# Moving the place at which split weights begin inside their tiles

## The chip, the cores and the metric

The kernel runs on one core of one Trainium2 chip. The number that counts is the device time of one execution in microseconds; three runs of the kernel before gave 1131.67, 1130.79 and 1130.77 us, so the median is 1130.79 us. A separate execution was profiled; everything that is said of single instructions comes from it. Its own time was 1131.15 us, of which 1129.4 us lie between the first and the last instruction.

## The reference

A decoder trunk of two layers on 512 tokens with 1024 features. Layer 0 mixes with a gated delta rule (six heads, chunks, short convolutions), layer 1 with sliding-window attention (twelve heads, sinks); both layers also attend to 256 memory tokens. After each mixer comes an output projection and a gated feed-forward part. Cut to what this case touches:

```python
def swiglu(h, w_gate_up, w_down):
    gu = h @ w_gate_up
    return (jax.nn.silu(gu[..., :D_FF]) * gu[..., D_FF:]) @ w_down

for layer in range(DEPTH):
    h = rms_norm(x, ln_mix[layer])
    ...                                   # mixer: projections of h, recurrence or attention
    x = x + jnp.concatenate([mix_out, mem_o], axis=-1) @ w_out[layer]
    x = x + swiglu(rms_norm(x, ln_ffn[layer]), w_gate_up[layer], w_down[layer])
    if layer == N_A_LAYERS - 1:
        kv = rms_norm(x, ln_kv) @ w_kv    # keys and values that layer 1 reads
return rms_norm(x, ln_final)
```

Here `D_MODEL` is 1024, `D_FF` is 2816, and all arrays are 32-bit floats. Nearly all arithmetic is in products of the activations with weight matrices.

## The kernel before

Activations are kept transposed: features on the 128 partitions, the 512 tokens along the free dimension. Every float32 operand of a large product is split into two parts, `h` (rounded to the type float32r, written by ScalarE at line 140) and `l` (the rest, written by VectorE at line 153), and one product becomes three matrix instructions, `whi` by `h`, `whi` by `l` and `wlo` by `h` (`mm3`, line 198). In each of them a 128 by 128 block of weights is loaded into TensorE and the activation streams past it.

There are two kinds of weights.

Whole projection tiles. `weight` (line 182) loads 128 output columns of a matrix, 1024 rows deep, as a tile of 128 by 1024 (two tiles of 768 and 640 in the down projection), splits it into a pair of tiles tagged `whi` and `wlo`, and `mm3` uses 512 bytes of a partition, 128 numbers, at a time. The activations that stream past are 512 tokens wide. 2478 matrix instructions of the program are of this kind. The tiles rotate over three buffers, so the next pair is split while the last one is used. The pair of tiles is 1152 numbers wide (`part`, line 195: `D + P`), 128 more than a weight needs, and a projection's weights begin at the first number.

Quarter weights. In the feed-forward part, the gate and up projections of two column tiles are computed together by a scheme with seven products for eight (`quarters`, line 1275): weights and activations are cut into halves, sums of the halves are formed by DMAs with addition, VectorE and ScalarE, and seven products of a 128 by 512 block of weights with 256 tokens follow, each of twelve matrix instructions. Nineteen such groups a layer, 38 in all, make 38 x 7 x 12 = 3192 matrix instructions. Their split weights go to a ring of six places (`ring`, line 1131): three pairs of tiles, two places in each, 512 numbers apart. Each place is a view of 512 numbers within the tile that begins `shift[0]` numbers after the place's start; `begin` sets `shift[0]` to `P - 8`, that is 120 numbers or 480 bytes, before its first product. Two places share one tile, so a place that is written with another shift can overlap its neighbour.

Tiles of 128 by 512 and 128 by 1024 are multiples of 512 bytes a partition, so in the built program the projections' weights and the activations they meet begin at the same position within a block of 512 bytes, and the quarter weights begin 480 bytes further on. In this document that difference, the weights' start less the activation's start within 512 bytes, is called the lag: 0 for the projections and 480 for the quarters. In the first 32 us, memory keys and values are made from other tiles and with lags of 128 and 384. At the end of layer 1 (from 1103.66 us) the last output tiles are made in pieces of 256 tokens with a lag of 0.

A scheduler orders each engine's instructions from the program's order and its dependences. Two views of one tile depend on each other when their bytes overlap. Each engine runs its own list in order.

Of the kernel before, what the change touches and what calls it, by code (L numbers as in the profile page):

```python
# [18 lines left out]
P = 128  # L19
# [8 lines left out]
FT = DFF // P  # L28
# [58 lines left out]
class Builder:  # L87
    def __init__(self, tc, a):
        self.tc, self.nc, self.a = tc, tc.nc, a
        self.n = 0  # L90
        self.valued, self.turned, self.scaled, self.behind = None, [], None, None
        self.scalings = []
        self.table, self.table_ins, self.table_users = None, None, []


# [86 lines left out]
    def weight(self, src, eng=None, raw=None, parts=1, pool=None, tags=("whi", "wlo"), bufs=3, after=None):  # L182

        raw = self.load(src) if raw is None else raw
        n = raw.shape[1]
        hi, lo = (self.part(tag, bufs, pool)[:, :n] for tag in tags)
        for i in range(parts):
            s = slice(i * n // parts, (i + 1) * n // parts)
            self.split(raw[:, s], hi[:, s], lo[:, s], eng or self.weng)
            if after is not None:  # L190
                for ins, other in zip((self.copied, self.low), after):
                    self.nosync(ins, other)
        return hi, lo
# [905 lines left out]
    def ffn(self, fp, xp, layer, h, apool, rope=False):  # L1099
# [4 lines left out]
        acts, sums, open_pairs, places, waiting, shift, sized = [], [], [], [], [], [0], []  # L1104
# [34 lines left out]
        def begin(f, up, by, tag, bufs, then):  # L1139

            o = [self.t(fp, [P, T], F32, tag, bufs) for _ in range(2)]
            steps = self.quarters(fp, [col(f + i, up) for i in range(2)], sums, by, o, ring)
            shift[0] = P - 8
            next(steps)
            while waiting:
                x = waiting.pop()
                self.nosync(self.fn(x, x, AF.Silu), self.held)
            end()
            next(steps)
            open_pairs.append((steps, then, o))  # L1150
            return o

        def end():
            if open_pairs:
                steps, then, o = open_pairs.pop()
                next(steps, None)
                for x in o:
                    then(x)
# [8 lines left out]
        for f0 in (0, half):  # L1167
# [7 lines left out]
            for f in range(f0 + 1, f0 + half, 2):  # L1175
                if f == 1:
                    g = []
                    for i in range(2):
                        for _ in range(2 - i):
                            sums.append(self.token_sums(fp, layer, len(sums), h))  # L1180
                        g.append(gate(f + i))
                    sums.append(self.token_sums(fp, layer, len(sums), h))
                else:
                    g = begin(f, 0, (self.rstd, self.rstd), "fg", 4, lambda x: self.fn(x, x, AF.Silu))
                begin(f, 1, g, "fu", 3, put)
# [432 lines left out]
```

## Time and profile before

| | |
|---|---|
| median of three runs | 1130.79 us |
| profiled execution | 1131.15 us, span 1129.4 us |
| TensorE (PE) busy | 1119.9 us, 99% of the span, 7339 instructions |
| weight loads (PEld) busy | 986.1 us, 87% |
| VectorE (DVE) busy | 827.6 us, 73% |
| ScalarE (ACT) busy | 634.4 us, 56% |
| granted TensorE clock | 0.998 |

An instruction of TensorE shows as two records, a weight load on the row PEld and a product on the row PE. Products are pipelined: the record of a 512-wide one lasts about 0.39 us, though the next starts some 0.23 us after it. So the duration in a row is no cost; what a matrix instruction costs is the distance from its start to the next start, and this document reads pace from start times. In the view by stretches, "x" counts the instructions that touch a stretch.

### The profile page before, as it was taken

What the parts mean: (1) busy time and instruction counts of PE and PEld (TensorE: products, weight loads), DVE (VectorE), ACT (ScalarE), POOL (GpSimd) and SP (SyncE); (2) the same over time, 40 slices, a digit from 0 to 9 for tenths busy, and PEclk for the clock granted to TensorE, in tenths of its full rate; (3) what the DMA queues carried; (4) which work ended last, traced back from release to release, by engine and by line L of the source; (5) the groups of instructions that cost most, each with busy time, mean ns of one, the idle gap of its engine ahead of it and who ended that gap; (6) DMA issues with size and microseconds to landing.
All of it is one profiled execution on the core that took longest, in us unless ns stands there. A gap on an engine that the chain in (4) does not pass through costs nothing.

```text
span 1129.4 us, 19330 instructions
## 1 busy us (share of the span) xinstructions
PE 1119.9 (99%) x7339; PEld 986.1 (87%) x7339; DVE 827.6 (73%) x1553; ACT 634.4 (56%) x1285; POOL 73.2 (6%) x91
## 2 busy tenths in 40 slices
PE   9999999999999999999999999999999999999997
PEld 8888778887899988899988887788999988999986
DVE  7676976577888975588955877839999634889643
ACT  8588664456566632366643555856666422666434
POOL 0000000000021001011000000000111000111001
PEclk9999999999999999999999999999999999999999
DMA  8344252234567536377533321116687533776232
GB/s 314 109 153 149 95 131 86 85 113 145 174 167 195 143 111 169 102 191 195 134 89 102 132 75 38 53 43 180 158 201 185 144 103 105 173 190 156 77 103 87
DMA packets 72401, 151.15 MB, mean 134 GB/s; under 512 B 16956, under 2 KB 18516, under 8 KB 72308
## 3 DMA queue, kind: packets, MB, share of 16 engines
q1 hardware_dynamic: 60884, 129.21, 36.3%
q0 software_dynamic: 11136, 20.45, 11.2%
q8 instruction: 57, 0.93, 0.3%
q14 instruction: 36, 0.29, 0.1%
q10 hardware_dynamic: 288, 0.26, 0.1%
HBM read 142.94 MB, written 6.96 MB: 133 GB/s over the span
## 4 chain that ended last, share of the span: by engine, by line
PE 96%; DVE 2%; ACT 1%; DMA 0%; issue 0%; DVEq 0%; SPq 0%; ACTq 0%
PE pj L146 46%; PE g L146 38%; PE sc L146 6%; PE qk L146 3%; PE pt L146 2%; PE pt L150 1%; PE g L150 1%; DVE big L153 1%; DVE qv L156 0%; DVE btmp L153 0%; DMA early<-in_early 0%; DVE wlo L153 0%; ACT sm L134 0%; DVE T L153 0%; DVE gcr L153 0%
## 5 line engine op out<-in xcount | busy, mean ns | idle before, releaser
L140 ACT ACTIVATE whi<-wraw 128x512 fp32r<-128x512 f32 (+3 forms) x318 | 235.3, 748 | 240.6 <-PE pj L146 164.0
L153 DVE TENSOR_TENSOR wlo<-wraw,whi 128x512 fp32r<-128x512 f32 (+3 forms) x318 | 262.8, 837 | 92.7 <-ACT whi L140 85.2
L146 PE MATMUL pj<-h,whi 128*128 128x512 f32 (+1 forms) x652 | 256.4, 395 | 0.0
L146 PE MATMUL pj<-l,whi 128*128 128x512 f32 (+1 forms) x652 | 254.4, 390 | 0.0
L146 PE MATMUL pj<-h,wlo 128*128 128x512 f32 (+1 forms) x652 | 254.0, 390 | 0.0
L146 PE MATMUL g<-T,whi 128*128 128x256 f32 x1216 | 216.8, 279 | 0.0
L146 PEld LDWEIGHTS g<-T,whi 128*128 128x128 f32 x1216 | 185.1, 188 | 1.3 <-DVE fu L156 1.3
L146 PE MATMUL g<-T,wlo 128*128 128x256 f32 x608 | 169.7, 279 | 0.0
L146 PEld LDWEIGHTS pj<-h,whi 128*128 128x128 f32 x652 | 122.4, 188 | 28.0 <-issue 4.1
L146 PEld LDWEIGHTS pj<-h,wlo 128*128 128x128 f32 x652 | 122.5, 188 | 25.4 <-issue 0.9
L146 PE MATMUL g<-l,whi 128*128 128x256 f32 (+1 forms) x500 | 144.5, 289 | 0.0
L146 PE MATMUL g<-h,whi 128*128 128x256 f32 (+1 forms) x500 | 144.4, 289 | 0.0
L146 PE MATMUL g<-h,wlo 128*128 128x256 f32 (+1 forms) x500 | 144.4, 289 | 0.0
L146 PEld LDWEIGHTS pj<-l,whi 128*128 128x128 f32 x652 | 122.6, 188 | 23.6 <-DVE l L1468 0.3
L146 PEld LDWEIGHTS g<-T,wlo 128*128 128x128 f32 x608 | 114.3, 188 | 0.0
L146 PEld LDWEIGHTS g<-h,whi 128*128 128x128 f32 x500 | 94.0, 188 | 1.9
L146 PEld LDWEIGHTS g<-l,whi 128*128 128x128 f32 x500 | 93.9, 188 | 1.9
L146 PEld LDWEIGHTS g<-h,wlo 128*128 128x128 f32 x500 | 93.9, 188 | 1.8
L1286 POOL DMA_DIRECT2D ws<-in_wgu x38 | 33.5, 881 | 733.0 <-DMA ws<-in_wgu 399.1
L140 ACT ACTIVATE whi<-ws 128x512 fp32r<-128x512 f32 x76 | 48.0, 631 | 42.0 <-PE g L146 35.6
L153 DVE TENSOR_TENSOR wlo<-ws,whi 128x512 fp32r<-128x512 f32 x76 | 52.0, 684 | 5.9 <-ACT whi L140 5.9
L1287 POOL DMA_DIRECT2D ws<-in_wgu x38 | 34.2, 900 | 196.4 <-DVE wlo L153 71.4
(421 smaller groups left out, 1683.2 us busy)
## 6 DMA issues: line engine op xcount, KB each, us to landing
wraw<-in_wgu SPq DMA_DIRECT2D x50, 512.0 KB, 4.4
ws<-in_wgu SPq DMA_DIRECT2D x76, 256.0 KB, 3.4
ws<-in_wgu POOLq DMA_DIRECT2D x76, 256.0 KB, 4.5
wraw<-in_win SPq DMA_DIRECT2D x26, 512.0 KB, 3.6
wraw<-in_wdn SPq DMA_DIRECT2D x32, 384.0 KB, 3.1
wraw<-in_wdn SPq DMA_DIRECT2D x32, 320.0 KB, 2.9
wraw<-in_wgu SPq DMA_DIRECT2D x38, 256.0 KB, 4.0
wraw<-in_wout SPq DMA_DIRECT2D x16, 512.0 KB, 3.6
```

The costliest lines, as they stand in the source:

```text
L140: self.copied = self.nc.scalar.activation(out, in_, AF.Copy, **kw).ins
L146: return self.nc.tensor.matmul(out, lhsT, rhs, start=start, stop=stop, skip_group_check=more).ins
L150: return self.nc.tensor.transpose(out, in_, self.ident[:k, :k]).ins
L153: return eng.tensor_tensor(out=out, in0=a, in1=b, op=op).ins
L1286: nc.gpsimd.dma_start(s1, a22, accum_op=ALU.add)
L1287: nc.gpsimd.dma_start(s3, a21, accum_op=ALU.add)
```

## The change

Two things move, and nothing else is edited. In `weight`, a projection's split weights now begin `at` numbers into their tiles; `at` is 0 for the first four tiles that are made, 8 for the next four, and so on up to 120, and then 0 again: 32 bytes more each four tiles. Tiles of a pool of their own keep their start. In `begin`, the shift of the quarter weights is 80 numbers (320 bytes) for all 19 groups of layer 0, and in layer 1 16, 24, 84, 76, 112 and 48 numbers for three groups each and 48 for the last.

In terms of the lag: of the 2478 matrix instructions of whole projections, 2412 get a lag other than 0, in steps of 32 bytes from 32 to 480. The 1596 quarter instructions of layer 0 go from 480 to 320. Those of layer 1 go to 64 (240 instructions), 96 (252), 336 (264), 304 (240), 448 (252) and 192 (348).

```diff
-        self.scalings = []
+        self.scalings, self.cuts, self.pairs = [], 0, 0
...
         raw = self.load(src) if raw is None else raw
         n = raw.shape[1]
-        hi, lo = (self.part(tag, bufs, pool)[:, :n] for tag in tags)
+        at = 0
+        if pool is None:
+            at = self.cuts // 4 * 8 % P
+            self.cuts += 1
+        hi, lo = (self.part(tag, bufs, pool)[:, at:at + n] for tag in tags)
...
             steps = self.quarters(fp, [col(f + i, up) for i in range(2)], sums, by, o, ring)
-            shift[0] = P - 8
+            shift[0] = 80 if self.pairs < FT - 3 else (16, 24, 84, 76, 112, 48, 48)[(self.pairs - FT + 3) // 3]
+            self.pairs += 1
             next(steps)
```

The engines' lists are the same before and after, but for a few swaps of neighbours in layer 1. The largest stands in the second half of layer 1, where the shift falls from 112 to 48 between the two places of one tile, `whi_10071`. The names are: `g` the accumulators, `T` and `h` halves of activations and their sums, `whi` and `wlo` the ring's tiles. On TensorE the piece of the difference reads:

```order
 L146 MATMUL g_10710<-T_8392,wlo_10072 128x256
+L146 MATMUL g_10710<-T_8283,whi_10067 128x256
+L146 MATMUL g_10710<-T_8284,whi_10067 128x256
 L146 MATMUL g_10839<-h_8032,whi_10071 128x256
 L146 MATMUL g_10839<-l_8033,whi_10071 128x256
+L146 MATMUL g_10841<-T_8283,whi_10067 128x256
+L146 MATMUL g_10841<-T_8284,whi_10067 128x256
+L146 MATMUL g_10841<-T_8283,wlo_10068 128x256
```

The product into `g_10839` was the next one after that of `g_10710`; now two instructions of another product stand between them, and nine more (the first three are shown) stand after its first two. On ScalarE, at the same place:

```order
 L140 ACTIVATE fs_10777<-g_10710 128x256
-L140 ACTIVATE whi_10069<-wraw_10829 128x512 x2
+L140 ACTIVATE whi_10069<-wraw_10829 128x512
 L140 ACTIVATE h_10889<-fu_10698 128x512
+L140 ACTIVATE whi_10071<-wraw_10829 128x512
+L140 ACTIVATE whi_10069<-wraw_10829 128x512
```

The copy that fills the second place of `whi_10071` stood seven rows earlier and now comes after the product that reads the first place, with which it shares 64 columns.

## Prediction

> **What bounds the kernel now.** I read the page from the top: busy shares, the slices with the granted clock, the chain that ended last.
>
> ```profile
> PE 1119.9 (99%) x7339; PEld 986.1 (87%) x7339; DVE 827.6 (73%) x1553; ACT 634.4 (56%) x1285; POOL 73.2 (6%) x91
> PEclk9999999999999999999999999999999999999999
> PE 96%; DVE 2%; ACT 1%; DMA 0%; issue 0%; DVEq 0%; SPq 0%; ACTq 0%
> PE pj L146 46%; PE g L146 38%; PE sc L146 6%; PE qk L146 3%; PE pt L146 2%; PE pt L150 1%; PE g L150 1%; DVE big L153 1%; DVE qv L156 0%; DVE btmp L153 0%; DMA early<-in_early 0%; DVE wlo L153 0%; ACT sm L134 0%; DVE T L153 0%; DVE gcr L153 0%
> ```
>
> TensorE holds 96% of the chain, 46% with projections (`pj`) and 38% with quarters and a few others (`g`), at a full clock. So a nanosecond more or less per matrix instruction goes almost whole into the time. Next, the pace, from stretches that hold one kind of instruction (the columns are time, then busy time and count of PE, PEld, DVE, ACT, POOL, then clock and DMA):
>
> ```profile
> 320.00:400.00 80.00, 80.00 (x688) 80.00 (x687) 72.86 (x132) 51.24 (x99) 12.22 (x14) 1.00 0.69 170
> 475.00:570.00 95.00, 95.00 (x806) 94.56 (x805) 82.70 (x148) 59.52 (x115) 13.10 (x15) 1.00 0.64 159
> 414.50:466.00 51.50, 51.50 (x229) 42.65 (x228) 31.84 (x48) 12.42 (x16) 3.68 (x4) 1.00 0.52 144
> 33.00:47.00 14.00, 14.00 (x62) 11.40 (x61) 9.19 (x15) 4.14 (x7) 2.39 (x4) 1.00 0.38 132
> ```
>
> The first two are quarter products: about 686 starts in 80 us (688 less those that only reach in), 116.7 ns each, and the same in 95 us. The third is a down projection, 512 tokens wide: 226.7 ns. VectorE, ScalarE and the DMAs are busy in all of them, and the pace doesn't waver, so it isn't set by them. The fourth is also 512 wide, but groups with lags 0 and 288 alternate: 14.39 us over 62 is 232 ns. It is the only long stretch that shows 512-wide products with another lag.
>
> How many instructions there are follows from groups by form:
>
> ```profile
> L146 PE MATMUL g<-T,whi 128*128 128x256 f32 x1216 | 216.8, 279 | 0.0
> L146 PE MATMUL g<-T,wlo 128*128 128x256 f32 x608 | 169.7, 279 | 0.0
> L146 PE MATMUL g<-l,whi 128*128 128x256 f32 x456 | 127.3, 279 | 0.0
> L146 PE MATMUL g<-h,whi 128*128 128x256 f32 x456 | 127.3, 279 | 0.0
> L146 PE MATMUL g<-h,wlo 128*128 128x256 f32 x456 | 127.3, 279 | 0.0
> ```
>
> That is 3192 quarter instructions, as the code has it. Now the pace by lag; each pair of rows is the first and last start of an unbroken run.
>
> ```profile
> 330.97 0.40 PE L146 MATMUL g<-T,whi 128*128 128x256 f32 x2
> 332.37 0.28 PE L146 MATMUL g<-h,whi 128*128 128x256 f32 x1
> ...
> 1104.02 0.28 PE L146 MATMUL pj<-h,whi 128*128 128x256 f32 x1
> 1107.50 0.28 PE L146 MATMUL pj<-ac10h,wlo 128*128 128x256 f32 x1
> ...
> 18.08 0.28 PE L146 MATMUL sc<-mh,wlo 128*128 128x256 f32 x1
> 20.60 0.28 PE L146 MATMUL sc<-mh,wlo 128*128 128x256 f32 x1
> ...
> 29.92 0.28 PE L146 MATMUL pj<-whi,ml 128*128 128x256 f32 x1
> 32.17 0.28 PE L146 MATMUL pj<-wlo,mh 128*128 128x256 f32 x1
> ```
>
> 256 wide: lag 480, 12 steps in 1.40 us, 116.7 ns. Lag 0 (the pieces at the end), 29 steps in 3.48 us, 120.0 ns. Lag 128, 21 steps in 2.52 us, 120.0 ns. Lag 384, 19 steps in 2.25 us, 118.4 ns. So the place seems to matter, by up to 3.3 ns, and the quarters now stand at the best of the four lags that the trace shows.
>
> 512 wide there is a second thing to see, at lag 0:
>
> ```profile
> 649.42 0.40 PE L146 MATMUL pj<-l,whi 128*128 128x512 f32 x1
> 651.74 0.39 PE L146 MATMUL pj<-h,wlo 128*128 128x512 f32 x1
> 654.69 0.39 PE L146 MATMUL pj<-h,whi 128*128 128x512 f32 x1
> ...
> 421.68 0.39 PE L146 MATMUL pj<-h,whi 128*128 128x512 f32 x1
> 429.16 0.39 PE L146 MATMUL pj<-h,whi 128*128 128x512 f32 x1
> ```
>
> After a break the first ten steps take 2.32 us, 232 ns each; the next thirteen 2.95 us, 226.9; and in the down projection 33 steps take 7.48 us, 226.7. The stream of products is restless first and then settles, and a restless product costs 5.3 ns more. Ten of them cost 0.05 us.
>
> **The change, part by part.** It removes and adds no instruction; it moves addresses. What could cost is the copy and subtraction that write the weights, the pace of TensorE, and waits.
>
> Writing at another place I cost at nothing. The quarter weights, written 480 bytes into the block, take as long as activations written at its start:
>
> ```profile
> L153 DVE TENSOR_TENSOR wlo<-wraw,whi 128x512 fp32r<-128x512 f32 x190 | 127.6, 688 | 16.9 <-ACT whi L140 12.1
> L153 DVE TENSOR_TENSOR l<-fu,h 128x512 fp32r<-128x512 f32 x32 | 21.9, 686 | 2.1 <-ACT h L140 1.0
> L140 ACT ACTIVATE whi<-wraw 128x512 fp32r<-128x512 f32 x190 | 116.8, 627 | 63.1 <-PE g L146 41.7 <-PE pj L146 14.3 <-DVE wraw L153 3.2
> L140 ACT ACTIVATE h<-fu 128x512 fp32r<-128x512 f32 x32 | 20.3, 633 | 19.9 <-DVE fu L153 11.8 <-DVE fu L156 8.1
> ```
>
> 688 against 686 ns, and 627 against 633. Both engines wait for TensorE in these stages, so 10 ns more would be covered; were that cover gone, 190 copies would cost 2 us.
>
> Quarters of layer 0, lag 320, 1596 instructions: no row has this lag. The nearest is 384, 118.4 ns; I take 1.8 ns more than now, 2.9 us. The ends are 120.0 ns (5.3 us more) and, since nothing shows that 480 is the best of all lags, as much the other way (5.3 us less).
>
> Quarters of layer 1: lags 64 and 192 (588 instructions) lie next to 0 and 128, both 120.0 ns: 3.3 ns more, 1.9 us. Lags 96, 336 and 304 (756) I give the 1.8 ns of lag 384: 1.4 us. Lag 448 (252) lies between 384 and 480: 0.9 ns, 0.2 us. Together 3.5 us; ends 5.3 us more and 5.3 us less.
>
> Projections, 2412 instructions at a lag other than 0. If a stream at any lag settles as at lag 0, they cost nothing. If at other lags it doesn't, each costs 5.3 ns, 12.8 us, which is what the stretch at 33 us looks like. That stretch changes lag every few instructions, whereas a place now holds for four tiles, some 100 instructions, ten times what settling took. I take a third of them as restless: 4.3 us. At each of 31 changes of place the stream may be restless for ten products, 0.05 us: 1.6 us, of which a third is already in; 1.1 us. Sum 5.4 us. The lower end is a gain: lag 0 is the dearest lag 256 wide; were it so 512 wide, other lags would save up to 3.3 ns, 8.0 us.
>
> One wait is added in layer 1, where the shift falls from 112 to 48 within `whi_10071` (the order above). ScalarE's copy must now wait for the last product with `whi` of the neighbour place. TensorE then has one instruction of that product and two of the next, 0.35 us, before it needs the copy, which takes 0.63 us and a handover: about 0.4 us of stop. Behind the copy on ScalarE stand two more copies for products that come over 1 us later, so nothing else is late; VectorE's subtraction, 0.69 us, ends beside the nine instructions that were moved ahead. Bounds 0.2 and 1.0 us. Where the shift rises, a place overlaps one that was used five products earlier, 7 us: free.
>
> Sum: 2.9 + 3.5 + 5.4 + 0.4 = 12.2 us. On the profiled execution's 1131.15 us that is 1143.35; the median of the runs is 0.36 us less, so I predict 1143.0 us.
>
> **The rivals.** Places don't matter. The four lags come from different parts of the program, with other tiles and other neighbours; the spread of 3.3 ns could belong to these. Then only the 0.4 us of the wait are left: 1131.2 us. Against it speaks that lag 480 gives 116.7 ns with every kind of half (`T`, `h`, `l`) and in stretches 150 us apart, so neighbours hardly matter there. The Trainium skill, in "TensorE: Matmul & The Clock Gate" (Step-by-step: what each phase is for), says that TensorE has two independent read ports and that loading the next weights takes no bandwidth from the running product; by that rule the place could not matter and this rival would be right, with the same 1131.2 us. The trace speaks against it as far as 116.7 and 120.0 ns for one shape do.
>
> Other lags are better for the projections. The mechanism: 256 wide, lag 0 costs 3.3 ns more than 480; the 512-wide products run beside the same weight loads, so lag 0 may cost them the same. With the full 3.3 ns on all moved projections (8.0 us less), half the loss on the quarters (3.2 us) and the wait, 1131.15 - 8.0 + 3.2 + 0.4 - 0.36 gives 1126.4 us. It decides if the moved projections run below 226.7 ns by more than the quarters lose: 6.8 us over 2412 is 2.8 ns, or 1.5 ns if the quarters lose half. For it: lag 0 is the worst seen 256 wide. Against it: the only 512-wide stretch with another lag is the slowest.
>
> Nothing settles. Projections at 232 ns throughout and quarters at 120.0: 12.8 + 10.6 + 0.4 on 1130.79 gives 1154.6 us. For it: the stretch at 33 us and two of four lags. Against it: that stretch mixes lags.
>
> **How the numbers follow.** Forecast, both kinds somewhat slower, 1136 to 1150 us: 0.55. Nothing settles: 0.17. Places don't matter: 0.09. Other lags better: 0.19, of which 0.02 ends within 0.2% of the time before. A difference of 0.2%, 2.3 us, is about what a measurement of this kernel can tell from no change. So faster 0.17, same 0.11, slower 0.72. The range goes from 1127 to 1156 us: it takes in the slow case and all but the far part of the fast one, leaving out about a tenth on each side. The likeliest case alone has 1136 (quarters at half their term, projections with only the 31 changes of place) to 1150 (quarters at 120.0 ns, projections two thirds restless).
>
> **What would show it.** Right: quarter runs of twelve in layer 0 that take more than the 1.40 us of now, near 1.42; another length in layer 1 for each place; down projections in which some tiles keep 7.48 us for 33 instructions and others take up to 7.66; near 1018 us a stop of TensorE of some 0.4 us that ScalarE's copy ends. Durations of copies and subtractions would stay within 10 ns. Wrong: quarters at 1.40 us in layer 0, or below; down projections below 7.48 us; or a stop of more than 1 us at places where the shift rises. What would make the forecast fail is that lags 320 and those between 32 and 480 are simply not like the ones I could see.

## The result and the profile after

The changed kernel takes 1142.07 us in the median of three runs (1141.65 to 1143.23), against 1130.79 us before: 1.0099 times as long, with a 95% interval of 1.0076 to 1.0122. The profiled execution has a span of 1140.3 us, 10.9 us more than the 1129.4 us of before. My 1143.0 us is 0.9 us off, and the sum was right. Its terms were not: two errors, each over 5 us, cancelled.

The page of the changed kernel, first busy time, then the chain that ended last:

```profile
PE 1130.1 (99%) x7339; PEld 986.9 (87%) x7339; DVE 828.1 (73%) x1553; ACT 634.8 (56%) x1285; POOL 73.2 (6%) x91
...
PE 96%; DVE 2%; ACT 1%; issue 0%; DMA 0%; DVEq 0%; ACTq 0%
```

TensorE has the same 7339 instructions and is busy 10.2 us longer; VectorE and ScalarE differ by half a microsecond. So the loss lies in the distance between products, as foreseen. The groups of copies and subtractions that write the weights:

```profile
L153 DVE TENSOR_TENSOR wlo<-wraw,whi 128x512 fp32r<-128x512 f32 x190 | 127.9, 688 | 17.0 <-ACT whi L140 12.3
L140 ACT ACTIVATE whi<-wraw 128x512 fp32r<-128x512 f32 x190 | 116.8, 628 | 69.4 <-PE g L146 42.4 <-PE pj L146 17.3 <-DVE wraw L153 3.2
L153 DVE TENSOR_TENSOR wlo<-wraw,whi 128x1024 fp32r<-128x1024 f32 x66 | 80.2, 1219 | 26.6 <-ACT whi L140 26.3
L140 ACT ACTIVATE whi<-wraw 128x1024 fp32r<-128x1024 f32 x66 | 69.3, 1055 | 50.0 <-PE pj L146 43.3 <-DMA wraw<-in_wout 2.9 <-DMA wraw<-in_wkv 2.4
```

688 and 628 ns for the quarters, against 688 and 627 before; 1219 and 1055 ns for the whole tiles, against 1218 and 1054. Writing at another place costs nothing.

Now the pace, from stretches of the changed kernel (time, then busy time and count of PE, PEld, DVE, ACT, POOL, then clock and DMA). The first five hold quarter products, the last two down projections.

```profile
322.00:402.00 80.00, 80.00 (x682) 80.00 (x681) 72.26 (x131) 50.91 (x99) 12.07 (x14) 1.00 0.68 167
485.00:565.00 80.00, 80.00 (x709) 80.00 (x708) 73.72 (x134) 52.45 (x102) 13.12 (x15) 1.00 0.75 183
812.00:832.00 20.00, 20.00 (x179) 20.00 (x179) 19.93 (x38) 11.89 (x25) 3.50 (x4) 1.00 0.79 200
837.00:862.00 25.00, 25.00 (x211) 25.00 (x210) 23.09 (x42) 15.84 (x31) 4.37 (x5) 1.00 0.80 194
1000.00:1025.00 25.00, 25.00 (x215) 25.00 (x214) 20.55 (x37) 14.77 (x29) 4.27 (x6) 1.00 0.78 192
449.00:464.00 15.00, 15.00 (x66) 12.06 (x65) 5.88 (x8) 2.77 (x5) 0.00 (x0) 1.00 0.44 126
465.00:482.00 17.00, 17.00 (x76) 13.95 (x75) 8.68 (x12) 3.93 (x7) 0.88 (x1) 1.00 0.34 94
```

The first two rows are the surprise. Both are layer 0, both lag 320, both 80 us; one holds 682 products, the other 709. From start to start that is 117.8 ns and 113.3 ns, and each holds its pace to the end of its half. Before, both took 116.7 ns. The next rows are lag 64 (113.3 ns), 96 (120.0) and 448 (117.8). In the down projections lag 416 gives 15 us over some 64 steps, 233 ns by the starts, and lag 448 17 us over some 74, 229 ns, against 226.7 at lag 0.

From the starts of all 512-wide products of projections, with distances over 260 ns (waits) left out, the mean per lag in the changed kernel is:

| lag | ns per product |
|---|---|
| 0, 256 | 227.5, 227.4 (226.8 without the unsettled first ten) |
| 192, 448 | 230.1, 229.1 |
| 128, 384 | 232.2, 232.9 |
| 32, 64, 160, 224, 288, 320, 416, 480 | 233.1 to 233.5 |
| 96, 352 | 234.1, 234.1 |

Over 226.7 ns these add up to 13.1 us; the same sum was 2.3 us before. The projections lost 10.8 us. The quarters, summed in the same way (distances over 130 ns left out) against 116.7 ns, gained 0.3 us: layer 0 gained 1.9 us, layer 1 lost 1.6 us.

The stop where the shift falls is there, in the rows of TensorE and, second, VectorE:

```profile
1026.36 0.28 PE L146 MATMUL g<-T,wlo 128*128 128x256 f32 x1
1027.47 0.50 PE L146 MATMUL g<-T,whi 128*128 128x256 f32 x2 [0.84 <-DVE fu L156]
```

```profile
1025.79 0.69 DVE L153 TENSOR_TENSOR fu<-fu,fg 128x512 f32<-128x512 f32 x1
1026.40 0.69 DVE L153 TENSOR_TENSOR wlo<-wraw,whi 128x512 fp32r<-128x512 f32 x1
1027.00 0.42 DVE L156 SCALAR_TENSOR_TENSOR fu<-g,fs 128x256 f32<-128x256 f32 x1
```

1.11 us pass from start to start where 0.12 are normal. The wait that ends last is one for VectorE, not for ScalarE's copy. The two instructions that were moved ahead write into the accumulator that VectorE has yet to read; before, another product stood between and gave VectorE that time. VectorE reads it at 1027.00, behind a multiplication and a subtraction of 0.69 us each.

The copy was hardly earlier, though. Here are ScalarE's rows, and the product that needs the copy:

```profile
1026.51 0.63 ACT L140 ACTIVATE h<-fu 128x512 fp32r<-128x512 f32 x1 [0.69 <-DVE fu L153]
1027.05 0.61 ACT L140 ACTIVATE whi<-wraw 128x512 fp32r<-128x512 f32 x1
```

```profile
1027.81 0.29 PE L146 MATMUL g<-h,whi 128*128 128x256 f32 x1
```

The copy stands behind `h<-fu`, which starts only when VectorE's multiplication is done, and ends at 1027.66. Without the wait for VectorE this product would have been due at about 1026.71 and would have waited for the copy instead: an estimate from these rows gives a stop of about 1.0 us for the copy alone.

### The profile page after: what moved, and what is told of

Its sections match the earlier page's. It is cut to its first block, busy times and chain, and to the rows that moved or that the text cites. A ratio compares the mean times of both kernels' runs of the same rounds, so it can differ in the third digit from the quotient of the medians.

```text
span 1140.3 us, 19329 instructions
## 1 busy us (share of the span) xinstructions
PE 1130.1 (99%) x7339; PEld 986.9 (87%) x7339; DVE 828.1 (73%) x1553; ACT 634.8 (56%) x1285; POOL 73.2 (6%) x91
## 4 chain that ended last, share of the span: by engine, by line
PE 96%; DVE 2%; ACT 1%; issue 0%; DMA 0%; DVEq 0%; ACTq 0%
PE pj L146 46%; PE g L146 38%; PE sc L146 6%; PE qk L146 3%; PE pt L146 2%; PE pt L150 1%; PE g L150 1%; ACT T L140 0%; DVE wlo L153 0%; DVE qv L156 0%; DMA wraw<-in_wdn 0%; DVE big L153 0%; DVE btmp L153 0%; ACT whi L140 0%; DVE T L153 0%
## 5 line engine op out<-in xcount | busy, mean ns | idle before, releaser
L146 PE MATMUL pj<-l,whi 128*128 128x512 f32 (+1 forms) x652 | 257.1, 395 | 0.0
L146 PE MATMUL pj<-h,wlo 128*128 128x512 f32 (+1 forms) x652 | 256.6, 394 | 0.0
```

Source lines behind the costliest of these rows:

```text
L146: return self.nc.tensor.matmul(out, lhsT, rhs, start=start, stop=stop, skip_group_check=more).ins
```

## The experiments

**One half of the change at a time.** Quarters alone moved, then projections alone (both edits start from the changed kernel):

```diff
-            at = self.cuts // 4 * 8 % P
+            at = 0
```

> The kernel before with the new shifts of the quarter weights alone; projections stay at lag 0. Theory 'each lag has its own lasting pace' (read from the trace of after: quarters altogether 0.3 us below before, one stop of about 1.2 us at the place where the shift falls): +0.9 us, 1131.7 us. Rival, the terms of my prediction (2.9 + 3.5 + 0.4): +6.8 us, 1137.6 us.

```diff
-            shift[0] = 80 if self.pairs < FT - 3 else (16, 24, 84, 76, 112, 48, 48)[(self.pairs - FT + 3) // 3]
+            shift[0] = P - 8
```

> The kernel before with the moving place of the projections' weights alone; quarters stay at lag 480. Theory of a lasting pace by lag (summed over the 512-wide products of the trace of after, about 11.0 us more than at lag 0): 1141.8 us. Rival, the terms of my prediction (a third of the products restless, 31 changes of place, 5.4 us): 1136.2 us.

Quarters alone: 1136.47 us (1135.82 to 1138.01) against 1131.08, 1.0049 times (1.0035 to 1.0063), 5.4 us more. Projections alone: 1142.98 us (1142.94 to 1143.09), 1.0106 times (1.0092 to 1.0120), 11.9 us more. The second is near what a lasting pace by lag asks for. The first is not; it is nearer to my own terms. And 5.4 and 11.9 make 17.3 us, while both changes together cost 11.3 us. Stretches of the two kernels, first quarters alone (lag 320 twice), then projections alone (lag 480 four times):

```profile
325.00:405.00 80.00, 80.00 (x681) 80.00 (x680) 70.62 (x128) 49.43 (x94) 11.38 (x13) 1.00 0.69 165
482.00:562.00 80.00, 80.00 (x682) 80.00 (x681) 71.74 (x129) 50.36 (x98) 13.10 (x15) 1.00 0.74 178
```

```profile
325.00:405.00 80.00, 80.00 (x688) 80.00 (x688) 70.90 (x129) 50.06 (x96) 11.38 (x13) 1.00 0.70 173
485.00:565.00 80.00, 80.00 (x682) 80.00 (x681) 71.68 (x130) 50.45 (x97) 13.09 (x15) 1.00 0.74 178
815.00:895.00 80.00, 80.00 (x681) 80.00 (x681) 72.22 (x133) 49.18 (x96) 14.88 (x17) 1.00 0.81 191
975.00:1065.00 90.00, 90.00 (x773) 90.00 (x773) 79.36 (x143) 57.47 (x110) 13.09 (x15) 1.00 0.67 164
```

With the projections at lag 0 the second half of layer 0 runs at 117.8 ns, not at 113.3, though its own lag is 320 as in the changed kernel. And quarters whose place never moved run at 116.7 or at 117.8 ns, depending on the half, once the projections move. So the pace isn't a function of the quarters' lag alone. The sums agree: against 116.7 ns the quarters lose 3.8 us when moved alone and 1.8 us when only the projections move, and gain 0.3 us when both do; 5.9 us, which is the missing 6.0 us.

**Lag 64 everywhere.**

```diff
-            shift[0] = P - 8
+            shift[0] = 16
```

> The kernel before, but all quarter weights at a shift of 16 numbers, lag 64, the lag that showed 113.3 ns in 240 instructions of after. Theory of a lasting pace by lag: 3192 x 3.3 ns = 10.6 us less, 1120.2 us. Rival, that the 113.3 ns belong to those three groups, their place in layer 1 or their neighbours: between no change and a third of that, 1127 to 1131 us. My prediction (lag 64 is like its neighbours 0 and 128, 120.0 ns): 10.6 us more, 1141.4 us.

1134.16 us (seven runs, 1131.90 to 1134.98), 1.0025 times (1.0014 to 1.0035): slower, where a pace of lag 64 by itself promised 10.6 us. All four halves look like the first:

```profile
325.00:405.00 80.00, 80.00 (x682) 80.00 (x681) 70.63 (x129) 49.42 (x94) 11.35 (x13) 1.00 0.69 167
```

117.8 ns in each of them. The theory "one pace for each lag" falls for the quarters, and so do all three expectations in size. Six of the seven runs lie between 1133.66 and 1134.98 us; in the seventh, at 1131.90 us, some stretch may have run faster, which is not shown.

**The stop.**

```diff
-            shift[0] = 80 if self.pairs < FT - 3 else (16, 24, 84, 76, 112, 48, 48)[(self.pairs - FT + 3) // 3]
+            shift[0] = 80 if self.pairs < FT - 3 else (16, 24, 84, 76, 112, 112, 112)[(self.pairs - FT + 3) // 3]
```

> The changed kernel, but the last seven groups of layer 1 keep the shift 112 (lag 448) where it fell to 48 (lag 192), so that no place overlaps its neighbour there. The two lags showed paces within 0.2 ns. If the overlap makes the stop of 1.1 us at 1026 us: 1.1 us less, 1141.0 us, and no gap over 0.2 us there. My prediction's price of that wait: 0.4 us less, 1141.7 us. Rival, that the stop has another cause: 1142.1 us, and the gap stays.

1141.09 us, 1.0 us under the changed kernel's 1142.07. Runs spread by more than that (1140.87 to 1143.88), so the time alone proves little, but the place in the trace does; in this kernel the rows there read:

```profile
1026.46 0.28 PE L146 MATMUL g<-T,wlo 128*128 128x256 f32 x1
1026.57 0.28 PE L146 MATMUL g<-h,whi 128*128 128x256 f32 x1
```

0.11 us: no stop. The overlap made it, by moving instructions, at about 1.0 us.

**Does the tile just ahead choose?** Only the projection tile before each of the four halves is moved, to the lags that stood ahead of the two fast halves in the changed kernel (448 ahead of 320, 224 ahead of 64), and then exchanged.

```diff
-            ps = self.project(col(f, 0), h, "pj")
+            ps = self.project(col(f, 0), h, "pj", at=(112, 56)[layer] if f == 2 else 0)
...
-            up = self.projected(col(f0, 1), h, "g")
+            up = self.projected(col(f0, 1), h, "g", at=(112, 56)[layer] if f0 else 0)
...
-            shift[0] = P - 8
+            shift[0] = (80, 16)[layer]
```

> The kernel before, with quarters at lag 320 in layer 0 and 64 in layer 1, and only the one projection tile that runs just before each of the four long quarter stretches moved: to lag 448 in layer 0, to 224 in layer 1, the two pairs that ran at 113.3 ns in after. All other projections stay at lag 0. Theory 'the lag offers two paces, and the products just before choose one': 113.3 ns in all four stretches, 3192 x 3.3 = 10.6 us less, and 0.4 us more for the four moved tiles: 1120.9 us. Rival 'the choice comes from further back or by chance': 117.8 ns as with projections at 0, 3.5 us more: 1135.0 us.

> As the other, with the two lags of the tiles ahead exchanged: 224 ahead of quarters at 320, 448 ahead of quarters at 64. If any tile ahead whose own pace is not steady at 226.7 ns leads to the fast pace: 1120.9 us. If only the two pairs seen do: 117.8 ns throughout, 1135.0 us; one kind alone gives about 1128 us.

1134.98 us (1.0034, 1.0021 to 1.0047) and 1134.86 us (1.0032, 1.0020 to 1.0045). All eight halves run at 117.8 ns; the rival "from further back or by chance" is right. But a small row in the first of the two kernels pointed on. At the end of the first half of layer 0, twelve quarter products follow three products of a projection, and the first of the twelve takes longer: 215 ns in the changed kernel, 202 here and 208 with the lags exchanged, 205 in the kernel with the quarters alone moved. At lag 320 the rest of the twelve settle at 113.3 ns within five products behind 202, 208 and 215 ns, and run at 117.8 behind 205. So one lag has both paces at the same place of the program, and nanoseconds at the entry go with the choice.

The plainest case lies in two kernels shown already. The kernel without the fall (112 kept) is the same program as the changed one up to the second half of layer 1, so here the two differ as executions only. Rows of the twelve products, first of the changed kernel, then of the one without the fall:

```profile
409.82 0.39 PE L146 MATMUL g<-T,whi 128*128 128x256 f32 x2
410.73 0.28 PE L146 MATMUL g<-T,wlo 128*128 128x256 f32 x1
```

```profile
409.79 0.40 PE L146 MATMUL g<-T,whi 128*128 128x256 f32 x2
410.73 0.28 PE L146 MATMUL g<-T,wlo 128*128 128x256 f32 x1
```

Eight steps take 0.91 us in the one and 0.94 us in the other. The first of the twelve took 215 ns and the last ones run at 113.3; in the other it took 205 ns and they run at 117.8.

**Lag or place?** Everything allocated from the left side is put 64 bytes further on.

```diff
+        self.t(cp, [P, 16], F32, "rest")
         c = self.t(cp, [P, C_N], F32, "consts")
```

> The kernel before, with everything that is allocated from the left side (weights and most activations) 64 bytes further on, and the tiles of the right side, T and the activations 8 to 10 of the down projections, where they were. Theory 'the distance between weights and activation counts': gate and up projections stay at 226.7 ns, and only the 9 of 33 products of a down projection that meet a tile of the right side, now at lag 64, change. Theory 'the place of the weights counts': all 512-wide products run at 233.3 ns, as those at lag 64 did in after, 16 us more.

One down projection of this kernel, where `h` moved along with the weights and `ac8` to `ac10` did not:

```profile
417.65 0.39 PE L146 MATMUL pj<-h,wlo 128*128 128x512 f32 x1
...
419.01 0.39 PE L146 MATMUL pj<-h,wlo 128*128 128x512 f32 x1
...
421.96 0.39 PE L146 MATMUL pj<-ac8h,whi 128*128 128x512 f32 x1
...
424.06 0.39 PE L146 MATMUL pj<-h,whi 128*128 128x512 f32 x1
```

Six products of `h` take 1.36 us, 226.7 ns each, with weights that begin at the same position within 512 bytes as those of lag 64 in the changed kernel (233.4 ns). The nine products of `ac8` to `ac10`, at lag 64, take 2.10 us, 233.3 ns. The distance counts, not the place of the weights. The time was 1135.86 us, 1.0046 times (1.0030 to 1.0062): besides these, the quarter products with `T` now have lag 32 and run at 118.1 ns.

**Does a stream settle at another lag?** Projections stay at one place for good, lag 256 in the first part and 32 after it.

```diff
-            at = self.cuts // 4 * 8 % P
+            at = 64 if self.pairs < FT - 3 else 8
...
-            shift[0] = 80 if self.pairs < FT - 3 else (16, 24, 84, 76, 112, 48, 48)[(self.pairs - FT + 3) // 3]
+            shift[0] = P - 8
```

> Quarters at lag 480 as before; projections at one place that never changes: lag 256 up to the end of the quarters of layer 0 (1224 products 512 wide), lag 32 from there on (1254 products). Theory of a lasting pace: 226.7 ns at 256, 233.2 at 32, 8.2 us more, 1139.3 us, up to 1 us more if a quarter stretch is led to its slower pace. My prediction (a stream settles at any place, and the changes of place cost): 226.7 ns at both, no change but one, 1131.1 us.

1138.89 us, 1.0070 times (1.0055 to 1.0085), where a lasting pace asked for 1139.3. Down projections at 256, then at 32:

```profile
415.50:465.00 49.50, 49.50 (x220) 41.02 (x219) 30.43 (x46) 11.86 (x15) 3.55 (x4) 1.00 0.55 147
897.00:957.00 60.00, 60.00 (x259) 48.35 (x258) 21.04 (x26) 14.03 (x18) 0.00 (x0) 1.00 0.37 104
```

About 218 starts in 49.5 us, 226.7 ns each; 257 in 60 us, 233.3 ns, without a wavering, over a place that never changes. At lag 32 a 512-wide stream doesn't settle to 226.7 ns. One of the four quarter halves, at lag 480 like the others, ran at 117.8 ns in place of 116.7, which is 0.9 us of the time.

**Choosing the pace at will.** Lag 64 everywhere again, with one small extra instruction ahead of each group:

```diff
             w = ring()
             self.split(raw, *w)
+            if b == "11":
+                n = 32 + 4 * (self.pairs % (FT - 3))
+                self.pairs += 1
+                self.mm(ps[:, :n], w[0][:, :P], sums[0][b][0][:, :n])
```

> All quarters at lag 64 and projections at lag 0, as in the run that held 117.8 ns in its long stretches, but ahead of the first product of each of the 38 groups one more matrix instruction with the same weights stands, 32 tokens wide in a layer's first group and 4 tokens wider in each next one, up to 104; its result is overwritten. Nothing else moves. Theory 'a lag of 64 holds two paces, and the moment at which the stream enters chooses': some groups run at 113.3 ns and others at 117.8, and a width makes the same choice in both layers. Rival 'the pace is fixed by lag and by the program's earlier places': 117.8 ns in all long stretches as without the extra instructions. The extra instructions themselves cost 38 times 30 to 120 ns, 1 to 5 us, so the time alone does not decide: 1129 to 1139 us by the first, 1136 to 1139 us by the rival.

The one execution took 1134.01 us, with the extra instructions in it; the trace says more. Of the 38 groups 14 run at 113.3 ns and 24 at 117.8, each from its first ten products to its end, and the two layers agree in all 19 places: widths 32, 48, 60, 68, 80, 92 and 100 lead to the fast pace, the twelve others to the slow one. Three neighbouring groups of layer 0 and the same three of layer 1 (44, 48 and 52 wide):

```profile
348.00:356.00 8.00, 8.00 (x70) 8.00 (x70) 7.47 (x14) 5.51 (x11) 0.87 (x1) 1.00 0.82 196
358.00:366.00 8.00, 8.00 (x73) 8.00 (x73) 6.64 (x13) 5.65 (x11) 0.97 (x2) 1.00 0.70 194
368.00:376.00 8.00, 8.00 (x70) 8.00 (x70) 7.48 (x14) 5.64 (x11) 0.87 (x1) 1.00 0.80 185
832.50:840.50 8.00, 8.00 (x70) 8.00 (x69) 7.54 (x15) 5.45 (x11) 1.74 (x2) 1.00 0.87 203
842.50:850.50 8.00, 8.00 (x73) 8.00 (x72) 6.64 (x13) 5.65 (x11) 0.65 (x2) 1.00 0.80 198
852.50:860.50 8.00, 8.00 (x70) 8.00 (x69) 7.48 (x14) 5.64 (x11) 0.87 (x1) 1.00 0.90 208
```

Without the extra instructions all 38 groups ran at 117.8 ns. So lag 64 holds two paces, and what happens at the entry chooses between them; that it does so by the time that the extra instruction takes is the likeliest reading, and not shown apart. Each of the fourteen groups that came behind one at 113.3 ns fell to 117.8. The state in which the stream arrives may count too, but here these groups always had the same widths, so this run can't tell.

**The same for 512 tokens.** Quarters at lag 480, all projections at lag 32, an extra instruction ahead of each tile:

```diff
+        if start and ah.shape[1] == T:
+            n = 32 + 4 * (self.wide % 19)
+            self.wide += 1
+            self.mm(ps[:, :n], wh[:, s], ah[:, :n])
         self.head = self.mm(ps, wh[:, s], ah, start, False, more)
```

> Quarters at lag 480, all projections at the constant lag 32, and an extra matrix instruction, 32 to 104 tokens wide in turn, ahead of the first product of each 512-wide projection tile (90 extra instructions, some 0.13 us each where the tile isn't waited for, 12 us). Theory 'every lag holds a fast pace and a slow one': a part of the tiles, as the width of the extra instruction chooses, runs at 226.7 ns. Rival 'lag 32 holds only the slow pace for 512 tokens': 233.2 ns in all of them, whatever the width; then the loss of the projections in after is a matter of the lag alone, and no entry would have saved it. Time: about 1131.1 + 16 + 12 = 1159 us by the rival, down to 1143 us by the first.

1160.8 us in one execution. In some 70 tiles with enough unbroken products, the mean is 232.6 to 233.5 ns in every one, whatever the width. For 512-wide products lag 32 showed no fast pace.

**A faster version.** Lag 64, and the extra instruction only ahead of each half (32 wide ahead of the first, 68 ahead of the second):

```diff
+            if b == "11":
+                n = {0: 32, 9: 68}.get(self.pairs % (FT - 3))
+                self.pairs += 1
+                if n:
+                    self.mm(ps[:, :n], w[0][:, :P], sums[0][b][0][:, :n])
```

> All quarters at lag 64, projections at lag 0, and one extra matrix instruction ahead of the first quarter product of each half of a layer alone, four in all: 32 tokens wide ahead of the first half, 68 ahead of the second, the widths after which these halves began at 113.3 ns. If a stretch keeps the pace with which it begins: 3184 quarter instructions at 113.3 in place of 116.7 ns, 10.6 us less, and 4 times about 0.12 us for the extra instructions: 1131.1 - 10.1 = 1121.0 us. If the pace is lost after some instructions: 1121 to 1135 us, in proportion. If the choice is by chance: spread between runs of 3 us or more.

1125.81 us (1122.21 to 1126.68), 0.9947 times before (0.9934 to 0.9961). Its stretches:

```profile
320.00:400.00 80.00, 80.00 (x708) 80.00 (x707) 72.19 (x132) 51.85 (x102) 11.53 (x14) 1.00 0.72 178
478.00:558.00 80.00, 80.00 (x709) 80.00 (x708) 73.64 (x133) 52.15 (x102) 13.12 (x15) 1.00 0.74 181
818.00:880.00 62.00, 62.00 (x529) 62.00 (x528) 55.73 (x101) 39.65 (x77) 10.51 (x12) 1.00 0.79 190
958.00:1048.00 90.00, 90.00 (x797) 90.00 (x796) 80.62 (x147) 59.20 (x113) 13.12 (x15) 1.00 0.68 167
```

Three halves keep 113.3 ns. The first half of layer 1 begins with it too, but at 817.00 TensorE waits for VectorE, and from there it runs at 117.8 ns to the end, some 575 products, 2.5 us. From start to start the stop takes 0.47 us in place of 0.11, so the pace behind it costs seven times the 0.36 us of the stop itself.

```profile
816.53 0.28 PE L146 MATMUL g<-T,wlo 128*128 128x256 f32 x1
817.00 0.47 PE L146 MATMUL g<-T,whi 128*128 128x256 f32 x2 [0.19 <-DVE fg L156]
```

The last run tried to lead that stream back:

```diff
-                n = {0: 32, 9: 68}.get(self.pairs % (FT - 3))
+                n = {0: 32, 9: 68, 19: 32, 22: 48, 28: 68}.get(self.pairs)
```

> The same with a fifth extra instruction, 48 tokens wide, ahead of the fourth group of layer 1, one group after the place where TensorE stopped for VectorE in the last kernel and the stream came back at 117.8 ns. A width of 48 led from 117.8 to 113.3 ns in both layers before. If a stream that was lost can be led back so: some 5 groups of 84 instructions at 4.4 ns less, 1.8 us, in those executions that have the stop, 0.1 us for the instruction: median about 1124.1 us. If the stop is not there in an execution, the extra instruction finds 113.3 ns and may lead to 117.8, up to 2 us more. If the spread of 4.5 us between runs comes from this one stop, it shrinks below 2 us; if it has other sources, it stays.

1124.62 us (1122.61 to 1124.81), 0.9938 times (0.9924 to 0.9952). That is faster than both kernels, but no different from the last one by its interval, and not for the reason expected: in its profile the stream falls to 117.8 ns behind a stop at the same place (0.33 us from start to start) and stays there behind the extra instruction of 48.

```profile
825.00:880.00 55.00, 55.00 (x470) 55.00 (x469) 49.18 (x89) 34.91 (x68) 9.64 (x11) 1.00 0.79 186
```

So a width that chose the fast pace twice in one program did not in another. The spread between runs is smaller, 2.2 us for 4.5; whether the fifth instruction did that stays open.

## Why the prediction was right, and where its terms were wrong

| term | predicted | found in the changed kernel |
|---|---|---|
| writing at another place | 0 | 0 |
| quarters, layer 0 | +2.9 us | -1.9 us |
| quarters, layer 1 | +3.5 us | +1.6 us |
| projections | +5.4 us | +10.8 us |
| the added wait | +0.4 us | +1.0 us |
| sum | +12.2 us | +11.5 us |

The spans differ by 10.9 us. The 0.6 us between lie with the other products (memory, recurrence, attention): from start to start these 1620 records take 0.7 us less than before. Why they do was not followed.

What held: that TensorE's pace sets the time, that the place of the weights against the activation changes it, that copies cost nothing, and that one stop is added. The rival "places don't matter" is wrong: the same shape takes 226.7 and 233.3 ns in neighbouring rows of one tile. The Trainium skill, in "TensorE: Matmul & The Clock Gate" (Step-by-step: what each phase is for), gives TensorE two independent read ports, so that loading weights takes nothing from the running product. The trace disagrees with what the prediction drew from this, that the place can't matter; whether the weight loads are what slows a product here, no run shows.

By the prediction's own signs it was right and wrong at once. Twelve quarter products of layer 0 take 1.41 us in the first half, near the 1.42 that it named; in the second half they take 1.36 us, and "below" 1.40 was its sign of being wrong.

Projections, 5.4 against 10.8 us. The step that failed is the mechanism "the stream of products is restless first and then settles", carried from lag 0 to other lags with "I take a third of them as restless". In the run with constant places, lag 32 kept 233.2 ns over some 1200 products. Only 256 settles as 0 does. The end that I gave for no settling, 12.8 us, was nearer to the truth. The 31 changes of place, 1.1 us of my sum, aren't seen as a cost of their own: lag 32 averages 233.2 ns in the changed kernel too. The stretch near 33 us could not have told this. I read its 232 ns as the cost of another lag, but 46 of its 60 products have lag 0 and take 231.3 ns there, and the 14 at lag 288 take 230.0, less than the 233.1 that this lag shows in the changed kernel. Most likely it is a stream that the changes of lag kept from settling; it resembles the lasting pace only in size.

Quarters, +6.4 against -0.3 us. The step that failed is reading one pace for each lag from the nearest of four lags ("the nearest is 384, 118.4 ns"). Each of the four lags showed one pace in its long rows, and only a short row hinted at more: near 22 us of the kernel before, fourteen steps at lag 128 take 1.67 us, 119.0 ns, where the row that I read had 120.0. (There is a fifth lag as well: 24 products of the first 32 us have lag 96 and take 118.9 ns, within 0.5 ns of what I gave that lag.) In the changed kernel half of layer 0 fell on 113.3 ns. With the projections left at 0 the quarters lost 3.8 us, and with the stop 4.8 of the 5.4 us measured; there my 6.8 us would have been a fair forecast. So the quarters' gain came from an entry that nobody chose, and it made up for the projections.

The wait, 0.4 against 1.0 us. It came at the place named, and its size is my upper bound. Two steps were wrong. One is that ScalarE's copy ends the stop: the order showed two instructions moved ahead, and I had not asked what these wait for. They write into an accumulator that VectorE was still to read, so the wait that ends last is VectorE's, behind two instructions of 0.69 us. The other is the price of the copy itself, "0.63 us and a handover": the order shows `h<-fu` ahead of it on ScalarE, and with that in the way the copy alone would have cost about 1.0 us as well.

Of the rivals, "nothing settles" was right for most lags of the projections and wrong for the quarters. "Other lags better" was wrong for the projections, of which it spoke; it was the quarters that found a faster pace, in part. That the terms were bounded from both sides kept the result inside a range 29 us wide; the point itself was luck.

## What to carry to other kernels

When products follow each other without a gap, read the pace from start to start and compare it over stretches with one shape: 3% between two of them, with all other engines idle at times and the clock full, is a sign that the distance between the weights' and the activation's start may matter. Keep 512-wide float32r streams at the same position within 256 bytes, and measure before trusting a pace for narrower ones, since here a stream held either of two paces and fell from one to the other behind a short stop. When an order of instructions changes, ask of each one that moved ahead what its own output waits for, not only of those that were delayed.

## What the runs showed that was not expected

A stream of 256-wide products at lag 64 or 320 holds 113.3 or 117.8 ns, for up to 828 products; at lag 480 it is 116.7 or 117.8 ns, and at lag 96 it was 120.0 ns in the changed kernel and 117.3 with the quarters alone moved. The same program took both paces at one place in two executions. For 512-wide products, lags that lie 256 bytes apart agree within 1 ns (the table above). The distances follow patterns: 118, 118, 117 and so on with nine that make 1060 ns; 120, 113, 116, 118 with 467 ns for four; 113.3, 120.0, 226.7 and 233.3 ns by themselves. All these sums are multiples of 6.67 ns (159, 70, 17, 18, 34 and 35). So something goes in steps of that size, but no run here shows what, nor why, of the lags tried, 512-wide products have their best at 0 and 256 and 256-wide ones at 64 and 320. What happens at the entry chooses between the two paces, and behind one stop of 0.36 us the slower one cost 2.5 us.
